# The down projection of a gated MLP as seven half-size products (Strassen), with weight sums made by accumulating transfers

## The chip, the cores and the metric

The kernel runs on one core of one Trainium2 chip. TensorE (PE) multiplies, VectorE (DVE), ScalarE (ACT) and GpSimd (POOL) do the element work, SyncE (SP) issues most of the transfers, and 16 DMA engines carry them. The metric is the device time of one execution in microseconds (us), the median of several runs.

## The reference

One layer of a hybrid decoder at 512 tokens and width 1024: a mixing sub-layer of four branches, then a gated MLP with a short convolution on its gate. The change lies in the MLP, and almost all of it in its last product:

```python
def conv_gated_mlp(h, w_up, conv_w, conv_b, w_down):
    up = h @ w_up                                   # 1024 -> 2 * 3072
    val = up[..., :D_FF]
    gate = causal_dwconv(up[..., D_FF:], conv_w, conv_b)
    return (val * jax.nn.gelu(gate)) @ w_down       # 3072 -> 1024

h = rms_norm(x, g_mlp_pre[l])
y = conv_gated_mlp(h, ...)
x = x + rms_norm(y, g_mlp_post[l])                  # the output
```

All data are fp32. The inputs and weights come from DRAM and the output goes back there.

## The kernel before

**Products in three passes.** A number is cut into a "hi" part that TensorE takes in one pass and a "lo" remainder. A product is hi by hi, hi by lo of the activations, and lo of the weights by hi of the activations, so one fp32 matmul is three matmuls of 128x128 by 128x512. A weight block of 128x1024 (512 KB) is fetched into `wraw` (`wfetch`, L72, on SP's queue), its hi part is copied by ACT (`whi`, L81), and DVE subtracts to give the lo part (`wlo`, L82). `split` does the same for an activation (L96 on ACT, L97 on DVE). `wraw`, `whi` and `wlo` have three buffers each.

**The up projection** (L791) is 48 units `upu(u)` of 24 matmuls. For each of 24 column chunks i there is a gate unit and a value unit; ACT and DVE do the convolution and the Gelu of the gate, DVE multiplies by the value (`fc`, L841), and `split` writes the activations `aT` (hi and lo, feature by token).

**The down projection** (L852) takes 24 weight blocks. Block 2p+nh holds the feature chunks 2p and 2p+1 (two halves of 512 columns in the block) of output half nh. 576 matmuls add into eight PSUM banks `acc[t, nh]`, one for each 128 tokens t and output half nh. The last four blocks are kept in `wl`, so that the four token tiles end one after another and the norm of one lies under the matmuls of the next.

**The norm and the output**: for each t two squares with sums on ACT (`fjk`, L881), a product with the gain (`fyg`, L877), the reciprocal root in small steps (L119 to L130), a scaled add to the residual (L887), and two stores (L888). The gain `gmo` is loaded once (L814).

Each engine works through its instructions in order, and a transfer waits in the order of the queue that issues it: SP's queue for the weights, POOL's for `gmo` and the two convolution constants. A scheduler has put each engine's instructions in an order, which can differ from that of the code.

Of the kernel before, what the change touches and what calls it, by code (L numbers as in the profile page):

```python
# [50 lines left out]
def _body(ctx, tc, nc, D):  # L51
# [758 lines left out]


    fp = fx.enter_context(pool("ff"))
    gmo = fp.tile([128, DM], F32, name="gmo")
    nc.gpsimd.dma_start(out=gmo, in_=D["g_mlp_post"])  # L814
    fcw = fp.tile([128, 24, 3], F32, name="fcw")
    fcb = fp.tile([128, 56], F32, name="fcb")[:, :24]
    nc.gpsimd.dma_start(out=fcw, in_=D["ffn_conv_w"])
# [26 lines left out]
    acc = {(t, nh): (mmb if nh == 0 else axb)("dn") for t in range(4) for nh in range(2)}  # L844

    def down(t, nh, kb, w, parts=(0, 1)):
        ts_ = slice(t * 128, (t + 1) * 128)
        for p in parts:
            for k in (2 * kb, 2 * kb + 1):
                cs = slice(k % 2 * 512, k % 2 * 512 + 512)  # L850
                for a in ((0,) if p else (0, 1)):
                    PE.matmul(acc[t, nh], aT[a][:, k, ts_], w[p][:, cs], start=(k == a == p == 0), stop=(k == 23 and p == 1))  # L852
# [14 lines left out]
    for t in range(4):
        for nh in range(2):
            for kb in (10, 11):
                down(t, nh, kb, W[kb, nh])  # L870
    for t in range(4):
# [409 lines left out]
```

## Time and profile before

| | us |
|---|---|
| median of 3 runs | 1184.91 (1182.65 to 1185.02) |
| the profiled execution | 1185.61 |
| its span, first to last instruction | 1183.8 |
| PE busy | 1163.4 (98%) |
| DVE busy | 687.7 (58%) |
| ACT busy | 522.8 (44%) |
| POOL busy | 124.6 (11%) |

The span is what the trace covers; 1.8 us of the profiled execution's time lie around it. PE is almost always busy, so a wait on another engine counts only if PE stands still for it.

### The profile page before, as it was taken

The page shows a single profiled execution, that of the slowest core. Times are in us where ns is not written, and L with a number is a line of the kernel's source. Part 1 is how long each engine was busy: PE and PEld are TensorE (multiplying, and loading weights), DVE is VectorE, ACT ScalarE, POOL GpSimd, SP SyncE. Part 2 cuts the span into 40 slices and gives each one's busy share as a digit, 9 for nine tenths or more (in the row PEclk, how much of TensorE's full clock was granted, in tenths as well). Part 3 has the DMA queues.
Part 4 walks back from the last instruction along what each step waited for, and adds up shares of the span by engine and source line. Part 5 has one row for each costly group of instructions (what it writes and reads, how often), then busy time and mean ns, then how long its engine had stood idle before and what let it go on. Part 6 is the DMA issues. An engine that isn't in the chain of part 4 may idle for free.

```text
span 1183.8 us, 15153 instructions
## 1 busy us (share of the span) xinstructions
PE 1163.4 (98%) x5786; PEld 969.0 (82%) x5786; DVE 687.7 (58%) x1249; ACT 522.8 (44%) x869; POOL 124.6 (11%) x163
## 2 busy tenths in 40 slices
PE   8999999998999999999999999999999999999997
PEld 8977788877788887888888888898888888888886
DVE  6857794588888534486447465585545444432224
ACT  6678734553434235443543234455444443422122
POOL 3000200196651000000000000010000000000000
PEclk9999999999999999999999999999999999999999
DMA  7612442213223322223122323713232323333221
GB/s 288 215 59 71 151 141 63 68 52 96 78 82 114 100 89 67 86 77 112 61 80 64 107 87 118 267 38 107 92 102 92 107 90 94 102 92 104 91 88 71
DMA packets 44296, 120.21 MB, mean 102 GB/s; under 512 B 9630, under 2 KB 13808, under 8 KB 44224
## 3 DMA queue, kind: packets, MB, share of 16 engines
q1 hardware_dynamic: 42432, 115.73, 30.1%
q0 software_dynamic: 1072, 2.46, 0.7%
q10 hardware_dynamic: 720, 1.06, 0.2%
q8 instruction: 45, 0.74, 0.2%
q14 instruction: 27, 0.22, 0.1%
HBM read 115.21 MB, written 4.01 MB: 101 GB/s over the span
## 4 chain that ended last, share of the span: by engine, by line
PE 88%; DVE 7%; DMA 1%; issue 1%; ACT 1%; POOL 1%; DVEq 0%; SPq 0%; ACTq 0%; POOLq 0%
PE up L791 22%; PE gate L90 12%; PE dn L852 11%; PE prj L90 7%; PE glu L90 4%; PE v L90 3%; PE k L90 3%; PE q L90 3%; PE xa L90 3%; PE us L90 3%; PE xq L90 3%; PE ga L90 3%; PE wo L711 2%; PE kv L267 1%; PE kv L90 1%
## 5 line engine op out<-in xcount | busy, mean ns | idle before, releaser
L82 DVE TENSOR_TENSOR wlo<-wraw,whi 128x1024 fp32r<-128x1024 f32 (+1 forms) x198 | 230.6, 1168 | 276.9 <-ACT whi L81 137.3
L81 ACT CAST whi<-wraw 128x1024 fp32r<-128x1024 f32 (+1 forms) x198 | 194.7, 986 | 332.0 <-PE dn L852 71.2
L791 PE MATMUL up<-h2l,whi 128*128 128x512 f32 (+1 forms) x400 | 148.9, 377 | 0.0
L791 PE MATMUL up<-h2h,whi 128*128 128x512 f32 (+1 forms) x400 | 148.7, 376 | 0.0
L90 PE MATMUL gate<-hTh,whi 128*128 128x512 f32 x256 | 101.1, 395 | 0.0
L90 PE MATMUL gate<-hTl,whi 128*128 128x512 f32 x256 | 100.5, 392 | 0.0
L791 PE MATMUL up<-h2h,wlo 128*128 128x512 f32 (+1 forms) x400 | 93.6, 376 | 0.0
L791 PEld LDWEIGHTS up<-h2l,whi 128*128 128x128 f32 x400 | 75.2, 188 | 13.9
L791 PEld LDWEIGHTS up<-h2h,whi 128*128 128x128 f32 x400 | 75.3, 188 | 13.8
L791 PEld LDWEIGHTS up<-h2h,wlo 128*128 128x128 f32 x400 | 72.3, 188 | 13.7
L90 PE MATMUL gate<-hTh,wlo 128*128 128x512 f32 x256 | 63.6, 389 | 0.0
L852 PE MATMUL dn<-whi,aTh 128*128 128x512 f32 x160 | 62.2, 389 | 0.0
L852 PE MATMUL dn<-whi,aTl 128*128 128x512 f32 x160 | 62.2, 389 | 0.0
L90 PEld LDWEIGHTS gate<-hTh,whi 128*128 128x128 f32 x256 | 48.1, 188 | 9.9 <-issue 0.5
L90 PEld LDWEIGHTS gate<-hTh,wlo 128*128 128x128 f32 x256 | 47.9, 188 | 9.8
L90 PEld LDWEIGHTS gate<-hTl,whi 128*128 128x128 f32 x256 | 48.1, 188 | 9.4
L841 DVE TENSOR_TENSOR fc<-fc,up 128x512 f32<-128x512 f32 x24 | 16.5, 687 | 57.6 <-PE up L791 56.5
L852 PE MATMUL dn<-wlo,aTh 128*128 128x512 f32 x160 | 39.5, 389 | 0.0
L290 DVE SCALAR_TENSOR_TENSOR th<-th,prj 128x512 f32<-128x512 f32 x24 | 16.4, 685 | 37.1 <-PE prj L90 36.8
L838 DVE SCALAR_TENSOR_TENSOR fc<-gs,fcw,fc 128x512 f32<-128x512 f32 x48 | 36.1, 751 | 1.5
L852 PEld LDWEIGHTS dn<-whi,aTl 128*128 128x128 f32 x160 | 30.0, 188 | 6.2
L852 PEld LDWEIGHTS dn<-wlo,aTh 128*128 128x128 f32 x160 | 30.0, 188 | 6.2
(517 smaller groups left out, 2439.9 us busy)
## 6 DMA issues: line engine op xcount, KB each, us to landing
wraw<-w_in SPq DMA_DIRECT2D x74, 512.0 KB, 3.5
wraw<-ffn_w_up SPq DMA_DIRECT2D x48, 512.0 KB, 3.4
wraw<-ffn_w_down SPq DMA_DIRECT2D x24, 512.0 KB, 3.5
wraw<-proj SPq DMA_DIRECT2D x24, 384.0 KB, 3.0
wraw<-ssm_glu SPq DMA_DIRECT2D x12, 384.0 KB, 3.0
wraw<-w_out SPq DMA_DIRECT2D x8, 512.0 KB, 4.3
wraw<-mem_wk SPq DMA_DIRECT2D x6, 512.0 KB, 6.8
wraw<-mem_wv SPq DMA_DIRECT2D x6, 512.0 KB, 4.2
```

What stands on the lines that cost most here:

```text
L81: cut[:] = (S.copy(hi[:, :n], raw[:, :n]), V.tensor_tensor(out=lo[:, :n], in0=raw[:, :n], in1=f32(hi[:, :n]), op=ALU.subtract))
L82: V.tensor_tensor(out=lo[:, :n], in0=raw[:, :n], in1=f32(hi[:, :n]), op=ALU.subtract))
L90: last = PE.matmul(out, a[:, k * 128:(k + 1) * 128], x[i][:, k], start=(n == 0), stop=(n == 3 * nk - 1))
L267: done = PE.matmul(bv[t][:, :256], mT[a][:, 4 * kh + k, t * 128:(t + 1) * 128], w[:, cs], start=(kh == k == o == 0 and a == 1), stop=(kh = ...
L290: V.scalar_tensor_tensor(out=th, in0=th, scalar=1.0, in1=b, op0=ALU.add, op1=ALU.mult)
L711: PE.matmul(b, mT[k][a][:, ts_], w[p][:, k % 2, :], start=(k == a == p == 0), stop=(k == 7 and p == 1))
L791: PE.matmul(b[:, cs], a[:, k * 128:(k + 1) * 128], x[:, k, cs], start=(n == k == 0), stop=(n == len(order) - 1 and k == KC - 1))
L838: V.scalar_tensor_tensor(out=c, in0=gs[:, j:j + 512], scalar=fcw[:, i, j:j + 1], in1=c, op0=ALU.mult, op1=ALU.add)
L841: V.tensor_tensor(out=c, in0=c, in1=bv, op=ALU.mult)
L852: PE.matmul(acc[t, nh], aT[a][:, k, ts_], w[p][:, cs], start=(k == a == p == 0), stop=(k == 23 and p == 1))
```

## The change

The activations are split in two halves of tokens and, within each pair of feature chunks p (12 pairs), in the even and the odd chunk; the weights likewise in the even and odd chunk and the two output halves. Of the eight half-size products of such a 2x2 scheme seven remain (Strassen in Winograd's form): P1 to P7, of 12 pairs x 2 token tiles x 3 passes = 72 matmuls each, 504 in all.

- **Order on PE.** Stage A: for each p, P5 and P7 with the weight sum `tb`, then P6 and P4 with the sum `ta` (24 matmuls, one "step"). Stage B: P1 (72 matmuls). Stage C: P3 and P2 (144 matmuls), the last three pairs held back and done token tile by token tile.
- **Weight sums.** With w0, w1 the two blocks of p and c0, c1 their even and odd halves, `tb` is loaded in two pieces (L896, L897) and then two transfers on POOL's queue add w1[c0] to each half of it (L901, `accum_op`), 256 KB each. The two pieces of `wraw` (L898, L899) are added on DVE to give `ta` (L902, L903). `tb` and `ta` are split as other weights are. Stages B and C load their weights in pieces of 256 KB again.
- **Activation sums** are made in the up projection: for each even and odd i together there are twelve DVE instructions, eleven of 256 columns and one of 512, where there were four of 512. Four parts of each p (512 KB) go to DRAM (`late`, L863, SP's queue) and come back into their place `SA` by a transfer on POOL's queue (L954) once step p of stage A has read it.
- **Memory.** The up projection's activations `h2` now lie in a pool of their own that is closed after it; the four buffers of `tb` for p of 1 and more lie there, so their loads begin when the last matmul of the up projection has read `h2`. `tb` of p = 0 and `wraw` of the first pairs use the old `wraw` buffers.
- `gmo` is loaded behind stage A. The output is put together from P1 to P7 by DVE adds and ACT copies; the last ones (L989, L992) stand ahead of the last two token tiles' norms.

```diff
     fp = fx.enter_context(pool("ff"))
-    gmo = fp.tile([128, DM], F32, name="gmo")
-    nc.gpsimd.dma_start(out=gmo, in_=D["g_mlp_post"])
...
-    aT = tuple(fp.tile([128, 24, L], F32R, name="aT" + s) for s in "hl")
+    a11, s2 = (fp.tile([128, 12, 256], F32, name=n) for n in ("a11", "s2"))
+    S3 = fp.tile([128, 12, 2, 256], F32R, name="S3")
+    SA = fp.tile([128, 12, 4, 256], F32R, name="SA")
+    late = [dp.tile([128, 4, 256], F32, name="late%d" % p) for p in range(12)]
...
-        V.tensor_tensor(out=c, in0=c, in1=bv, op=ALU.mult)
-        split(aT[0][:, i], aT[1][:, i], c)
+        p = i // 2
+        if i % 2 == 0:
+            V.tensor_tensor(out=a11[:, p], in0=c[:, :256], in1=bv[:, :256], op=ALU.mult)
+            V.tensor_tensor(out=c[:, 256:], in0=c[:, 256:], in1=bv[:, 256:], op=ALU.mult)
+            V.tensor_tensor(out=c[:, :256], in0=a11[:, p], in1=c[:, 256:], op=ALU.subtract)
+            split(S3[:, p, 0], S3[:, p, 1], c[:, :256])
+            a21 = c[:, 256:]
+        else:
+            V.tensor_tensor(out=c, in0=c, in1=bv, op=ALU.mult)
+            t4 = x1p.tile([128, 1024], F32R, tag="wel", name="t4").rearrange("p (s n) -> p s n", s=4)
+            split(SA[:, p, 2], SA[:, p, 3], c[:, 256:])
+            split(t4[:, 2], t4[:, 3], c[:, :256])
+            V.tensor_tensor(out=c[:, 256:], in0=c[:, 256:], in1=a21, op=ALU.subtract)
+            split(SA[:, p, 0], SA[:, p, 1], c[:, 256:])
+            V.tensor_tensor(out=s2[:, p], in0=c[:, 256:], in1=a11[:, p], op=ALU.add)
+            V.tensor_tensor(out=c[:, :256], in0=c[:, :256], in1=s2[:, p], op=ALU.subtract)
+            split(t4[:, 0], t4[:, 1], c[:, :256])
+            nc.sync.dma_start(out=late[p], in_=f32(t4))
...
-    for kb in range(10):
-        for nh in range(2):
-            w = wload(D["ffn_w_down"][kb * 2 + nh], 1024)
-            for p in (0, 1):
-                for t in range(4):
-                    down(t, nh, kb, w, (p,))
...
+    for p in range(12):
+        wd = (D["ffn_w_down"][2 * p], D["ffn_w_down"][2 * p + 1])
...
+            tb = dnp.tile([128, 1024], F32, tag="wtb", name="wtb", bufs=4)
+        nc.sync.dma_start(out=tb[:, c0], in_=wd[0][:, c0])
+        nc.sync.dma_start(out=tb[:, c1], in_=wd[1][:, c1])
+        nc.sync.dma_start(out=raw[:, c0], in_=wd[1][:, c1])
+        nc.sync.dma_start(out=raw[:, c1], in_=wd[0][:, c1])
+        for c in (c0, c1):
+            nc.gpsimd.dma_start(out=tb[:, c], in_=wd[1][:, c0], accum_op=ALU.add)
+        V.tensor_tensor(out=ta[:, c0], in0=tb[:, c0], in1=raw[:, c0], op=ALU.add)
+        V.tensor_tensor(out=ta[:, c1], in0=raw[:, c1], in1=ta[:, c0], op=ALU.add)
...
+        sa = halves(s2[:, p])
+        split(*wb_, tb)
+        prods(P5, [SA[:, p, x] for x in (0, 1)], wb_, c0, f, l)
+        prods(P7, [S3[:, p, x] for x in (0, 1)], wb_, c1, f, l)
+        split(*wa, ta)
+        prods(P6, sa, wa, c0, f, l)
+        prods(P4, [SA[:, p, x] for x in (2, 3)], wa, c1, f, l)
...
+    for p in range(12):
+        if p % 2 == 0:
+            w = wparts(D["ffn_w_down"][2 * p][:, c0], D["ffn_w_down"][2 * p + 2][:, c0])
+        if p > 5:
+            reload()
+        prods(P1, halves(a11[:, p]), w, (c0, c1)[p % 2], p == 0, p == 11)
...
+    for r in range(2):
+        for n, (b, a, w) in enumerate(rest):
+            prods(P3, b, w, c1, False, n == 2, (r,))
+        V.tensor_tensor(out=x22[r], in0=x22[r], in1=P3[r], op=ALU.add)
+        for n, (b, a, w) in enumerate(rest):
+            prods(P2, a, w, c0, False, n == 2, (r,))
+        V.tensor_tensor(out=s1[r], in0=s1[r], in1=P2[r], op=ALU.add)
+        final(r, (s1[r], x22[r]))
```

On POOL's queue the last three transfers of before stand at the end of its program; the gain, the taps and the bias of the convolution:

```order
L814 DMA gmo_7195<-g_mlp_post 128x1024
L817 DMA fcw_7197<-ffn_conv_w 128x72
L818 DMA fcb_7198<-ffn_conv_b 128x24
```

At the same place of the changed kernel the load of the gain is gone from its place (it comes back behind stage A), and 24 accumulating transfers and 12 reloads follow the two constants. The accumulating ones are those of L901, for p = 0 (`wraw_9113`) and p = 1 to 5 here (`x2`: one for each half); those of L954 bring `late` back into `SA`:

```order
L901 DMA wraw_9113<-ffn_w_down 128x512 x2
L901 DMA wtb_9160<-ffn_w_down 128x512 x2
L901 DMA wtb_9207<-ffn_w_down 128x512 x2
L954 DMA SA_7205<-late0_7206 128x1024
L901 DMA wtb_9254<-ffn_w_down 128x512 x2
L901 DMA wtb_9301<-ffn_w_down 128x512 x2
L901 DMA wtb_9348<-ffn_w_down 128x512 x2
L954 DMA SA_7205<-late1_7207 128x1024
L901 DMA wtb_9395<-ffn_w_down 128x512 x2
```

So the reload of p stands ahead of accumulating transfers of stage A, and waits there until step p is done.

On DVE, at the start of the down projection, before had the lo parts of weight blocks alone:

```order
L82 TENSOR_TENSOR wlo_9029<-wraw_9026,whi_9028 128x1024
L82 TENSOR_TENSOR wlo_9059<-wraw_9056,whi_9058 128x1024
L82 TENSOR_TENSOR wlo_9089<-wraw_9086,whi_9088 128x1024
L82 TENSOR_TENSOR wlo_9119<-wraw_9116,whi_9118 128x1024
```

Now the adds stand between them. Here `wtb_9160`, `wta_9159`, `wlo_9172` and `wlo_9170` belong to p = 1 (`wlo_9172` is the lo part of its `tb`, `wlo_9170` that of its `ta`), and `wtb_9207`, `wta_9206`, `wlo_9219`, `wlo_9217` to p = 2:

```order
L902 TENSOR_TENSOR wta_9206<-wtb_9207,wraw_9205 128x512
L97 TENSOR_TENSOR wlo_9172<-wtb_9160,whi_9171 128x1024
L902 TENSOR_TENSOR wta_9159<-wtb_9160,wraw_9158 128x512
L903 TENSOR_TENSOR wta_9206<-wraw_9205,wta_9206 128x512
L903 TENSOR_TENSOR wta_9159<-wraw_9158,wta_9159 128x512
L97 TENSOR_TENSOR wlo_9170<-wta_9159,whi_9169 128x1024
L97 TENSOR_TENSOR wlo_9219<-wtb_9207,whi_9218 128x1024
L97 TENSOR_TENSOR wlo_9217<-wta_9206,whi_9216 128x1024
```

The first add of p = 2, which reads the accumulated `wtb_9207`, stands ahead of the lo part that step 1 multiplies with.

In stage B, on DVE, the lo parts of `a11` (`asl`, two buffers, one for each of the 12 pairs) alternate with the lo parts of the weights, one for two pairs:

```order
L97 TENSOR_TENSOR asl_9742<-a11_7202,ash_9741 128x256
L97 TENSOR_TENSOR asl_9760<-a11_7202,ash_9759 128x256
L966 TENSOR_TENSOR x210_9681<-x210_9681,p6_9109 128x512
L966 TENSOR_TENSOR x211_9682<-x211_9682,p6_9110 128x512
L82 TENSOR_TENSOR wlo_9816<-wraw_9812,whi_9815 128x1024
L97 TENSOR_TENSOR asl_9771<-a11_7202,ash_9770 128x256
L97 TENSOR_TENSOR asl_9790<-a11_7202,ash_9789 128x256
```

So an `asl` of every second pair stands behind a `wlo` in the queue.

## Rows read from the trace of the kernel before

**Rows 1.** The page: span; busy time and share by engine; chain by engine.

```profile
span 1183.8 us, 15153 instructions
PE 1163.4 (98%) x5786; PEld 969.0 (82%) x5786; DVE 687.7 (58%) x1249; ACT 522.8 (44%) x869; POOL 124.6 (11%) x163
...
PE 88%; DVE 7%; DMA 1%; issue 1%; ACT 1%; POOL 1%; DVEq 0%; SPq 0%; ACTq 0%; POOLq 0%
```

**Rows 2.** Chain that ended last: start us, length us, its two last steps.

```profile
793.87 252.14 PE up L791 x1161
1046.01 130.57 PE dn L852 x576
```

**Rows 3.** Windows in up and down: length, busy us by engine, PEclk, DMA share, GB/s.

```profile
880.00:901.80 21.80, 21.80 (x98) 18.06 (x97) 10.47 (x15) 9.26 (x12) 0.00 (x0) 1.00 0.30 98
1060.00:1080.00 20.00, 20.00 (x90) 16.57 (x89) 4.90 (x4) 4.22 (x4) 0.00 (x0) 1.00 0.31 100
```

**Rows 4.** Groups by line and form from 790 us on: busy, mean ns, idle before.

```profile
L82 DVE TENSOR_TENSOR wlo<-wraw,whi 128x1024 fp32r<-128x1024 f32 x64 | 78.3, 1223 | 137.3 <-ACT whi L81 71.8 <-PE dn L852 63.2 <-PE up L791 2.2
L81 ACT CAST whi<-wraw 128x1024 fp32r<-128x1024 f32 x64 | 67.4, 1053 | 125.8 <-PE dn L852 71.2 <-PE up L791 54.5
...
L841 DVE TENSOR_TENSOR fc<-fc,up 128x512 f32<-128x512 f32 x24 | 16.5, 687 | 57.6 <-PE up L791 56.5 <-ACT fc L839 1.2
L97 DVE TENSOR_TENSOR aTl<-fc,aTh 128x512 fp32r<-128x512 f32 x24 | 16.4, 684 | 0.7 <-ACT aTh L96 0.7
...
L96 ACT CAST aTh<-fc 128x512 fp32r<-128x512 f32 x24 | 14.9, 622 | 34.3 <-DVE fc L841 34.3
```

**Rows 5.** Groups by form, whole span: weight splits of 256 columns.

```profile
L82 DVE TENSOR_TENSOR wlo<-wraw,whi 128x256 fp32r<-128x256 f32 x8 | 3.4, 424 | 11.1 <-PE gate L90 8.0 <-issue 3.0
...
L81 ACT CAST whi<-wraw 128x256 fp32r<-128x256 f32 x8 | 3.3, 407 | 12.5 <-PE gate L90 12.2 <-PE prj L90 0.4
```

**Rows 6.** Window while a 256 KB output store runs, columns as before.

```profile
1175.50:1176.20 0.70, 0.70 (x5) 0.56 (x3) 0.06 (x1) 0.00 (x0) 0.00 (x0) 1.00 1.04 386
```

**Rows 7.** DMA in 10 to 20 us: packets, MB, share of 16 engines.

```profile
q1 hardware_dynamic: 1130, 4.11, 102.0%
```

**Rows 8.** DMA issues: queue, count, KB each, median us to landing.

```profile
wraw<-ffn_w_down SPq DMA_DIRECT2D x24, 512.0 KB, 3.5
...
out_dram<-x SPq DMA_DIRECT2D x4, 256.0 KB, 2.1
...
ab<-ab POOLq DMA_DIRECT2D x2, 256.0 KB, 3.9
...
gmo<-g_mlp_post POOLq DMA_DIRECT2D x1, 512.0 KB, 3.7
```

**Rows 9.** Groups on POOL: the issue of a transfer there.

```profile
L487 POOL DMA_DIRECT2D ab<-ab x6 | 3.3, 551 | 133.6 <-DVE nmc L541 108.3 <-DVE z L1077 20.3 <-DVE KT L1136 5.0
```

**Rows 10.** Timeline of SP: start us, length of four issues.

```profile
1.18 1.85 SPq L201 DMA_DIRECT2D memT<-memT  x4
```

**Rows 11.** Timeline from 1176 us: the end of the kernel.

```profile
1176.66 0.60 ACT L881 ACTIVATE fjk<-dn 128x512 f32<-128x512 f32 x1 [2.03 <-PE dn L852]
...
1177.38 0.21 DVE L119 TENSOR_SCALAR fot<-cols 128x1 f32<-128x1 f32 x1 [1.82 <-ACT fjk L881]
1177.52 0.68 DVE L877 TENSOR_TENSOR fyg<-dn,gmo 128x512 f32<-128x512 f32 x1
1177.63 0.20 ACT L120 ACTIVATE foy<-fot 128x1 f32<-128x1 f32 x1 [0.28 <-DVE fot L119]
1178.11 0.15 DVE L123 RECIPROCAL foy<-foy 128x1 f32<-128x1 f32 x1
...
1180.43 0.33 SPq L888 DMA_DIRECT2D out_dram<-x  x1
```

**Rows 12.** Windows of 1 us near the start: columns as in the windows above.

```profile
7.00:8.00 1.00, 0.42 (x3) 0.33 (x3) 1.00 (x4) 1.00 (x4) 0.00 (x0) 1.00 1.03 383
...
9.00:10.00 1.00, 1.00 (x6) 1.00 (x6) 1.00 (x4) 0.83 (x2) 0.00 (x0) 0.50 1.02 418
...
11.00:12.00 1.00, 1.00 (x8) 1.00 (x8) 0.95 (x2) 0.77 (x2) 0.00 (x0) 0.72 1.03 422
```

More of the change, by code (lines that the diff above doesn't have):

```diff
@@ L687, in _body @@
     x1 = [x1[:, t] for t in range(4)]
-    h2 = tuple(x1p.tile([128, KC, L], F32R, tag="h2" + s, name="h2" + s) for s in "hl")
     cols = x1p.tile([128, 128], F32, name="cols")
+    h2x = ExitStack()
+    h2p = h2x.enter_context(pool("h2p", side="right"))
+    h2 = tuple(h2p.tile([128, KC, L], F32R, name="h2" + s) for s in "hl")
     with pool("wo") as wo:
@@ L840, in _body @@
         bv = upu(2 * i + 1)
-        V.tensor_tensor(out=c, in0=c, in1=bv, op=ALU.mult)
-        split(aT[0][:, i], aT[1][:, i], c)
-    S.sqrt(warm, warm)
[L844 to L852, printed above, removed]
@@ L867, in _body @@
[L867 to L871, printed above, removed]
+        p = i // 2
[16 more added lines that the diff above has]
+            nc.sync.dma_start(out=late[p], in_=f32(t4))
@@ new lines, in _body, with halves, prods @@
+    S.sqrt(warm, warm)
+    h2x.close()
+    dnp = fx.enter_context(pool("dn", side="right"))
+    def halves(src):
+        t = tuple(fp.tile([128, 256], F32R, tag="a" + x, name="as" + x, bufs=2) for x in "hl")
+        split(*t, src)
+        return t
+    def prods(banks, a, w, cs, first, last, rs=(0, 1)):
+        n = [0, 0]
+        for lo in (0, 1):
+            for r in rs:
+                for x in ((0,) if lo else (0, 1)):
+                    PE.matmul(banks[r], a[x][:, r * 128:(r + 1) * 128], w[lo][:, cs], start=(first and n[r] == 0),
+                              stop=(last and n[r] == 2))
+                    n[r] += 1
@@ L872, in _body, with final @@
+    gmo = x1p.tile([128, 1024], F32, tag="weh", name="gmo")
+    nc.gpsimd.dma_start(out=gmo, in_=D["g_mlp_post"])
+    side = lambda nm: [dnp.tile([128, 512], F32, name="%s%d" % (nm, r)) for r in range(2)]
+    u2, q7, x21, x22 = (side(n) for n in ("u2", "q7", "x21", "x22"))
+    for r in range(2):
+        S.copy(u2[r], P5[r])
+        S.copy(q7[r], P7[r])
+    def final(t, src):
         sc = cols[:, 8 + 2 * t:10 + 2 * t]
@@ L888, in _body, with wparts @@
             (nc.sync if nh else nc.scalar).dma_start(out=D["out"][t * 128:(t + 1) * 128, cs], in_=x1[t][:, cs])
+    def wparts(x, y):
+        raw = wp.tile([128, 1024], F32, tag="raw", name="wraw")
+        nc.sync.dma_start(out=raw[:, c0], in_=x)
+        nc.sync.dma_start(out=raw[:, c1], in_=y)
+        return wload(None, 1024, raw)
+    rest = []
+    P1, P3, P2 = ([f(n) for _ in range(2)] for n, f in (("p1", axb), ("p3", axb), ("p2", mmb)))
+    s1 = x1p.tile([128, 1024], F32, tag="wel", name="s1")
@@ new lines, in _body, with reload @@
+    s1 = [s1[:, c0], s1[:, c1]]
+    back = iter(range(12))
+    def reload():
+        p = next(back, None)
+        if p is not None:
+            nc.gpsimd.dma_start(out=SA[:, p], in_=late[p])
+    for p in range(12):
[4 more added lines that the diff above has]
+        prods(P1, halves(a11[:, p]), w, (c0, c1)[p % 2], p == 0, p == 11)
+        if p in (2, 3):
+            V.tensor_tensor(out=x21[p - 2], in0=q7[p - 2], in1=P4[p - 2], op=ALU.add)
+        elif p in (4, 5):
+            V.tensor_tensor(out=x22[p - 4], in0=P6[p - 4], in1=u2[p - 4], op=ALU.subtract)
+        elif p in (6, 7):
+            V.tensor_tensor(out=x21[p - 6], in0=x21[p - 6], in1=P6[p - 6], op=ALU.subtract)
@@ new lines, in _body @@
+    for r in range(2):
+        S.copy(s1[r], P1[r])
+    for p in range(12):
+        w = wparts(D["ffn_w_down"][2 * p][:, c1], D["ffn_w_down"][2 * p + 1][:, c1])
+        reload()
+        b, a = ([SA[:, p, x] for x in y] for y in ((0, 1), (2, 3)))
+        if p < 9:
+            prods(P3, b, w, c1, p == 0, False)
+            prods(P2, a, w, c0, p == 0, False)
+        else:
+            rest.append((b, a, w))
+        if p in (1, 2):
+            r = p - 1
+            V.tensor_tensor(out=x22[r], in0=x22[r], in1=s1[r], op=ALU.subtract)
+            V.tensor_tensor(out=x21[r], in0=x21[r], in1=s1[r], op=ALU.add)
+            V.tensor_tensor(out=u2[r], in0=x22[r], in1=q7[r], op=ALU.subtract)
+        if p in (3, 6):
+            final(2 + p // 6, (x21[p // 6], u2[p // 6]))
@@ L889, in _body @@
+    for r in range(2):
+        for n, (b, a, w) in enumerate(rest):
[5 more added lines that the diff above has]
+        final(r, (s1[r], x22[r]))
     fx.close()
```

26 lines of the change are left out of this document (14 added, 12 removed).

## The prediction

> **What bounds the kernel now.** I read the page first: PE is busy for 98% of the span, and the chain that ended last is PE for 88% [rows 1]. DVE's 58% and ACT's 44% therefore cost something only where PE stands still for them. The chain's last steps say where the change acts: the up projection is one unbroken run of matmuls for 252.14 us, the down projection another for 130.57 us [rows 2]. So in both stages PE alone sets the time; 130.57 / 576 = 0.2267 us for one matmul. The windows show what is free beside it: per 21.8 us of the up projection DVE works 10.47 us and ACT 9.26; in 20 us of the down projection DVE works 4.9, ACT 4.2, and the DMA engines are 31% busy with 100 GB/s [rows 3]. A stage that gives PE less to do and the others more has to be judged by what these three then need.
>
> **Saved: matmuls.** 576 − 504 = 72 matmuls of the same shape, 72 x 0.2267 = **−16.3 us**. A step of stage A (24 matmuls) takes 5.44 us, twelve of them 65.3, stage B 16.3, stage C 32.6.
>
> **The up projection: 0.** For two chunks i DVE did 2 x 0.687 (L841) and 2 x 0.684 (lo parts) [rows 4]; now one of 0.687 and eleven of 256 columns, which the lo part of a 128x256 weight block prices at 0.424 [rows 5]. That is 5.35 in place of 2.74, so 10.47 + 2.6 = 13.1 us of 21.8. ACT makes five hi parts of 0.407 [rows 5] in place of two of 0.622 [rows 4], +0.8. Each store of 512 KB adds some 1.3 us of DMA time to engines that are 30% busy. PE's next unit needs none of this, only a free PSUM bank, which the multiply at the head of the chain frees as before; the 8 us that DVE still has idle are the cover. If it were gone, the 12 pairs would cost up to 2.6 us each; at 60% I see no reason.
>
> **Stage A: DVE and ACT have room.** A step needs on DVE two adds of 0.684, two lo parts of 1.223 and one of 0.424 = 4.2 us of 5.44; on ACT two copies of 1.053 and one of 0.407 = 2.5 [rows 4, 5].
>
> **Stage A: the transfers.** This is what decides. 256 KB at 386 GB/s, with all 16 engines busy (share 1.04), are 0.68 us of everything the DMA engines have [rows 6]; 4.11 MB in 10 us at 102% make 1.27 us for 512 KB [rows 7]. From the last matmul of the up projection (call it T; only then may `tb` of p ≥ 1 be loaded) until the accumulation for p = 11 has landed, these have to pass: 22 pieces of `tb` (15.0 us), 16 pieces of `wraw` for p = 4 to 11 (10.9), seven reloads that stand ahead in POOL's queue (8.9), the last `late` store (1.3), and 22 accumulating transfers. The first four make 36.1 us. The trace of before has no accumulating transfer. Its lower bound is a copy, 0.68 us (it cannot move less than its 256 KB), so 15.0 in all. It must however read the addend from DRAM and the old value from SBUF, 512 KB read for 256 KB written: the 512 KB row gives 1.27, twice the copy 1.36. An upper bound is three passes of a copy, 2.04. I take 1.27 to 1.36, since the row of 512 KB is the nearest to reading twice: 28 to 30 us, and 64 to 66 us in all.
>
> When is it needed? DVE, in the queue shown for step 1 and likewise later, makes the adds of p+2 ahead of the lo part of step p+1's `tb`. So step 10's third pass waits for the accumulation of p = 11, two adds and one lo part (2.6 us), and one landing (2.1 us for 256 KB on SP's queue [rows 8], of which 0.68 was counted). Step 10 would start at T + 54.4 and has 0.9 us of hi matmuls ahead; so the transfers must be done by about T + 51.4. Add 1 us in which the DMA engines idle after T (nothing can be accumulated before the first piece has landed). Lateness: copy 51.1 + 1 − 51.4 ≈ 0.7; at 1.27, 13.7; at 1.36, 15.6. I take **+14.6 us**. Most of it would show as PE waiting for `wlo` of the next step, spread over stage A.
>
> The Trainium skill has a rule on this, on the page "Collectives: The Full Stack", section "The bandwidth ceiling: the fold count and why AG ≠ RS ≠ AR": a reduce reads two sources for one write and was measured at about half of the copy's rate (62.28 against 32.35). That is for collectives; no run here shows it. By it alone an accumulating transfer is an estimated 1.3 us and the sum stays at about +2.5; by the copy's row it would be −5.9.
>
> **The transition into stage A** is part of this lateness when the transfers bind; with cheap ones it stands alone. At T SP issues `tb` for p = 1 and 2, 0.46 us apart [rows 10]; the third piece has landed at about T + 3.5 (2.1, then 0.68 for each further). POOL issues for 0.55 us [rows 9], and a 256 KB transfer of its queue took 3.9 us to land against 2.1 on SP's [rows 8]: T + 7.4. DVE's add of p = 2 (0.68), which stands ahead of step 1's `wlo_9172` (1.22), ends that at T + 9.3; PE wants it at 5.44 + 0.9 = T + 6.3. That is a wait of 3.0. Behind `wlo_9172` stand three adds (2.0) and ACT's copy (1.05), so `ta` is ready at T + 12.4, where PE has come to its products at 9.3 + 1.8 = 11.1: 1.3 more, and 0.4 for its lo part: 4.7. PE's granted clock fell to 0.50, 1.2 GHz of 2.4, two windows after one with PE busy for 0.42, and was at 0.72 two windows later [rows 12]; here the matmuls behind the first wait are partly covered by the second. With that and the hand-offs I take 6.2.
>
> **Stage B.** DVE has six weight lo parts (7.3), eleven `asl` (4.7) and eight adds of 512 (5.5): 17.5 us beside 16.3 of PE, so at least 1.2 late, and every second `asl` stands behind a lo part of 1.22 with only two buffers: up to some 5. I take **+3.0**. Stage C has one lo part in 2.72 us of matmuls: 0; the last five reloads (6.4 us) have stage B for it.
>
> **The end.** Before, ACT's last square started 0.08 us after the last matmul (1046.01 + 130.57 = 1176.58 [rows 2], 1176.66 [rows 11]) and DVE went on at 1177.38. Now an add out of PSUM (0.68, as `fyg`) comes first, and both squares follow it in series, 0.7 to 0.8 more. Before, `fyg` of 0.68 held the reciprocal back by some 0.28 (it started at 1178.11, where ACT's root had ended at 1177.83 [rows 11]); that now stands elsewhere. **+1.2 us**. The two stores and their landing stay (last issue at 1180.43 [rows 11]). `gmo`, 3.7 us from issue [rows 8], comes behind stage A and is needed 20 us later: 0.
>
> **Sum**: −16.3 + 14.6 + 3.0 + 1.2 = +2.5 on the profiled 1185.6 (0.7 above the median, within the runs), so **1188 us**.
>
> **Rivals.** (A) *The accumulating transfer costs hardly more than a copy.* Then stage A needs 51 us of transfers in 65 and only the transition is left: −16.3 + 6.2 + 3.0 + 1.2 = −5.9, **1180 us**. For it: engines that read and write at once might take the second read along, and nothing in the trace says they don't. Against: twice the bytes are read, and at full share time went with bytes [rows 6, 7]. It decides where 51.1 + 22(a − 0.68) − 50.4 = 12.1, at a = 1.20 us, 1.8 copies: just under my value. (B) *It costs nearly three copies, or POOL's queue is late in handing out its packets*: at 1.87 us for one the transfers take 77 us, the lateness is 26.8, the sum +14.7, **1200 us**. For it speaks POOL's queue landing 1.8 us later than SP's for the same 256 KB [rows 8]; against, POOL has nothing else to do, and 0.55 us an issue is far below 1.3. The page "SBUF — State Buffer" of the Trainium skill, in its note on the "DVE blocks DMA" trap, lets DVE copies in a two-port mode starve such a queue; the DVE work of stage A is adds and subtractions, which it does not count among them, and no run here shows it. (C) *Nothing waits*: the scheduler's order leaves slack that I have not seen, the clock holds, stage B hides: −16.3 + 1.2 + at most 3 ≈ −12, **1174 us**. Against it stands the first accumulation at T, which cannot land before about T + 6.
>
> **How the numbers follow.** The measurement tells some 0.2% (2.4 us) from no change. Forecast (accumulating costs 1.6 to 2.3 copies, 1184 to 1193): 0.46; A (below, 1179 to 1184): 0.31; B (1194 to 1204): 0.18; C: 0.05. Faster by over 0.2% (below 1182.5): most of A, and C, 0.34; within: 0.18 from the edge of A and the lower third of the forecast; slower: 0.48. The range takes A and half of B in: 1178 to 1201. The forecast's own is 1184 to 1193.
>
> **What would show it.** The down stage at 504 matmuls of about 0.227 us busy; in stage A a DMA share near 1 with PE waiting for `wlo` in most steps from 1 to 10, and the accumulating transfers on POOL's queue at twice a copy's packet time. With A the share would be near 0.8 and all waiting at step 1. Stage B should show short waits for `asl`, 1 to 5 us together, the end from the last matmul to the last instruction 1.2 us longer, and the up projection unchanged at 252 us. A longer up projection, or waits in stage C, would make me wrong for a cause not counted here.

## The result: 0.6% slower, and where the time went

The changed kernel takes 1190.84 us (median of 4 runs, 1189.92 to 1191.29) against 1184.95 of before: a ratio of 1.0059, 95% interval 1.0047 to 1.0071. That lies in the range and on the side that was forecast, 3 us above the point. The range went from 1178 to 1201 us and held faster kernels as well as slower ones, so being inside it says little; that the time also lies in the forecast's own 1184 to 1193 says more.

The page of the profile after, its busy times by engine and its DMA queues (packets, MB, share of 16 engines' span); `q0` is POOL's:

```profile
PE 1155.6 (97%) x5714; PEld 958.0 (81%) x5714; DVE 767.7 (65%) x1427; ACT 559.4 (47%) x953; POOL 152.5 (13%) x199
...
q1 hardware_dynamic: 52800, 131.47, 33.8%
q0 software_dynamic: 6256, 15.05, 5.1%
```

In before the chain ran through one unbroken row of matmuls up to the last of them [rows 2]. Now the chain that ended last has transfers in it (its long steps: start, length, step):

```profile
792.03 252.17 PE up L793 x1161
1050.56 8.36 DMA wtb<-ffn_w_down
1076.17 9.30 DMA wtb<-ffn_w_down
1090.97 7.74 DMA wtb<-ffn_w_down
1104.57 19.76 PE p L881 x78
1139.55 33.39 PE p L881 x145
```

The up projection still takes 252.17 us, so its activation sums cost nothing. What PE waited for in the down projection is in its timeline (start, length, form; in brackets the idle time before and what ended it):

```profile
1044.02 1.07 PE L881 MATMUL p<-whi,SA 128*128 128x512 f32 x4
...
1058.06 2.07 PE L881 MATMUL p<-whi,SA 128*128 128x512 f32 x4 [8.37 <-ACT whi L96]
...
1085.06 0.73 PE L881 MATMUL p<-wlo,SA 128*128 128x512 f32 x2 [0.83 <-DVE wlo L97]
...
1104.57 1.18 PE L881 MATMUL p<-wlo,SA 128*128 128x512 f32 x2 [2.27 <-DVE wlo L97]
...
1127.39 0.39 PE L881 MATMUL p<-whi,ash 128*128 128x512 f32 x1
...
1132.62 0.73 PE L881 MATMUL p<-whi,asl 128*128 128x512 f32 x2 [0.41 <-DVE asl L97]
...
1179.01 0.39 PE L881 MATMUL p<-wlo,SA 128*128 128x512 f32 x1
```

Stage A runs from 1044.02 to 1127.39 (its end is the first matmul of stage B): 83.4 us for 288 matmuls, 18.1 more than 288 x 0.2267. Of that, from the same timeline, step 0 to step 1 lost 8.6, step 1 another 3.1 (on a halved clock), step 5 1.2, step 6 0.5, step 8 4.2 (2.27 of waiting and again matmuls on a slow clock, 0.58 on the mean from 1104 to 1108). Steps that did not wait took 5.51 us as well, not 5.44. Stages B and C took 52.0 us, 3.0 over 216 x 0.2267. From the last matmul's end (1179.40) to the end of the span (1189.0) are 9.6 us; before it was 7.2 (1176.58 to 1183.8). So the down projection and the end got −16.3 + 18.1 + 3.0 + 2.4 = 7.2 us longer. In these two executions the up projection ended 2.0 us earlier after (1044.02 against 1046.01 [rows 2]), which makes the spans differ by 5.2 only; in the other profiled kernels here it ended between 1042.8 and 1045.1 though the code of their up projection is the same, so this shift is not taken for an effect of the change.

The windows (length, busy us by engine, PEclk, DMA share, GB/s) show the transfers at their limit through stage A, and the clock in the first wait:

```profile
1046.00:1118.00 72.00, 60.18 (x240) 47.10 (x240) 43.10 (x59) 26.74 (x33) 24.93 (x33) 0.91 1.08 307
...
1050.00:1055.00 5.00, 0.00 (x0) 0.00 (x0) 0.00 (x0) 0.00 (x0) 3.99 (x5) 0.84 1.06 274
1055.00:1060.00 5.00, 1.94 (x5) 1.56 (x6) 1.06 (x2) 1.04 (x1) 0.91 (x2) 0.50 1.12 282
```

The DMA share stands at 1.08 for 72 us, where before had 0.31 [rows 3]; but only 307 GB/s are counted, against 386 to 422 at full share [rows 6, 12]; the experiment with two loads below shows where the rest is. DVE was busy for 43 of the 72 us, so its sum of work isn't the bound. With PE standing still the granted clock fell to 0.50, 1.2 GHz, and PE's first products after the wait ran at that.

### The profile page after: what moved, and what is told of

Its sections match the earlier page's. It is cut to its first block, busy times and chain, and to the rows that moved or that the text cites. A ratio compares the mean times of both kernels' runs of the same rounds, so it can differ in the third digit from the quotient of the medians.

```text
span 1189.0 us, 15579 instructions
## 1 busy us (share of the span) xinstructions
PE 1155.6 (97%) x5714; PEld 958.0 (81%) x5714; DVE 767.7 (65%) x1427; ACT 559.4 (47%) x953; POOL 152.5 (13%) x199
## 4 chain that ended last, share of the span: by engine, by line
PE 86%; DVE 5%; DMA 5%; issue 2%; ACT 1%; POOL 1%; SPq 0%; DVEq 0%; POOLq 0%; ACTq 0%
PE up L793 22%; PE gate L90 14%; PE prj L90 8%; PE p L881 5%; PE glu L90 4%; DMA wtb<-ffn_w_down 4%; PE v L90 3%; PE k L90 3%; PE q L90 3%; PE xa L90 3%; PE us L90 3%; PE xq L90 3%; PE ga L90 3%; PE wo L713 2%; PE kv L267 1%
## 5 line engine op out<-in xcount | busy, mean ns | idle before, releaser
L82 DVE TENSOR_TENSOR wlo<-wraw,whi 128x1024 fp32r<-128x1024 f32 (+1 forms) x196 | 228.0, 1167 | 177.2 <-ACT whi L81 80.4
L881 PE MATMUL p<-whi,SA 128*128 128x512 f32 x192 | 53.9, 396 | 8.4 <-ACT whi L96 8.4
L881 PEld LDWEIGHTS p<-whi,SA 128*128 128x128 f32 x192 | 36.4, 190 | 16.7 <-ACT whi L96 8.8
L763 POOL TENSOR_TENSOR xn<-xn,gpr 128x512 f32<-128x512 f32 x2 | 3.4, 1701 | 275.3 <-ACT xn L762 275.3
L843 DVE SCALAR_TENSOR_TENSOR fc<-gs,fcw,fc 128x512 f32<-128x512 f32 x48 | 36.1, 751 | 1.7
L881 PE MATMUL p<-wlo,SA 128*128 128x512 f32 x96 | 32.0, 405 | 3.3 <-DVE wlo L97 3.1
L844 ACT ACTIVATE fc<-fc 128x512 f32<-128x512 f32 x24 | 15.2, 632 | 40.1 <-DVE fc L843 40.1
L901 POOL DMA_DIRECT2D wraw<-ffn_w_down x2 | 1.8, 1065 | 232.1 <-DMA wraw<-ffn_w_down 232.1
```

What stands on the lines that cost most here:

```text
L82: V.tensor_tensor(out=lo[:, :n], in0=raw[:, :n], in1=f32(hi[:, :n]), op=ALU.subtract))
L763: G.tensor_tensor(out=tt, in0=tt, in1=gpr[:, cs], op=ALU.mult)
L881: PE.matmul(banks[r], a[x][:, r * 128:(r + 1) * 128], w[lo][:, cs], start=(first and n[r] == 0), stop=(last and n[r] == 2))
L901: nc.gpsimd.dma_start(out=tb[:, c], in_=wd[1][:, c0], accum_op=ALU.add)
```

## The experiments

The table gives for each run the ratio to before with its interval, and from its PE timeline the length of stage A, of stages B and C, and of the stretch from the last matmul to the end of the span (without any wait at 0.2267 us a matmul: 65.3 and 49.0 us).

| run | ratio | A | B + C | end |
|---|---|---|---|---|
| before (130.57 in all) | 1 | | | 7.2 |
| the change | 1.0059 [1.0047, 1.0071] | 83.4 | 52.0 | 9.6 |
| e1_plain | 0.9995 [0.9986, 1.0005] | 75.4 | 52.7 | 9.6 |
| e2_two_loads | 1.0053 [1.0038, 1.0068] | 81.7 | 52.8 | 9.6 |
| e3_reload_late | 1.0038 [1.0024, 1.0053] | 78.5 | 55.3 | 9.6 |
| e4_dve_sums | 1.0022 [1.0013, 1.0032] | 78.7 | 51.6 | 9.6 |
| e5_early_tb1 | 1.0027 [1.0017, 1.0037] | 78.9 | 52.2 | 9.6 |
| e6_three_asl | 1.0061 [1.0043, 1.0079] | 85.3 | 49.9 | 9.6 |
| e7_squares_first | 1.0059 [1.0044, 1.0074] | 83.0 | 51.9 | 8.6 |
| e8_best | 0.9882 [0.9867, 0.9896] | 66.1 | 49.8 | 8.6 |
| e9_acc_placed | 1.0010 [1.0001, 1.0019] | 76.9 | 51.9 | 9.6 |
| e10_acc_placed_late | 1.0004 [0.9994, 1.0014] | 73.9 | 56.3 | 9.6 |

The median of before was 1183 to 1185 us over these sets of runs, so ratios are compared, not times. For each run the three lengths, less 130.57 + 7.2, give its difference to before within 1.5 us; the table holds nearly all that changed.

**What an accumulating transfer costs.** In e1 it is a plain load:

```diff
-            nc.gpsimd.dma_start(out=tb[:, c], in_=wd[1][:, c0], accum_op=ALU.add)
+            nc.gpsimd.dma_start(out=tb[:, c], in_=wd[1][:, c0])
```

> The 24 accumulating transfers become plain loads of the same 256 KB on the same queue, behind the same waits (the weight sum tb is therefore not made, the data are those of one addend). Theory (an accumulating transfer takes the DMA engines about two copies, and in stage A the DMA engines are the bound): some 22 x 0.7 = 15 us of DMA time go; the waits at steps 5, 6 and 8 (1.2 + 0.5 + 4.2 us) vanish and the first two (8.6 + 3.1) shrink to about 6, so about 11 us less, near 1180 us. Rival 1 (the bound is the chain load, POOL issue, landing, whatever the transfer does): 1190 +- 2 us, the same waits. Rival 2 (DVE's order, the adds of p+2 ahead of the lo part of p+1, is the bound): also 1190 +- 2 us.

Measured: 7.6 us off (1.0059 to 0.9995 of 1184), all in stage A, where the theory had 11 and both rivals none. The waits at steps 5, 6 and 8 are gone, as the theory had it. The losses at steps 0 and 1 fell by 2.2 us only (9.5 us in place of 11.7) and not to 6: there an effect other than the accumulate is at work. PE's first wait in e1:

```profile
1056.79 2.07 PE L881 MATMUL p<-whi,SA 128*128 128x512 f32 x4 [6.37 <-ACT whi L96]
```

POOL's queue and SP's over 72 us of stage A, in the change and then in e1 (packets, MB, share of 16 engines):

```profile
q0 software_dynamic: 4444, 10.43, 61.5%
q1 hardware_dynamic: 6262, 11.66, 46.3%
```

```profile
q1 hardware_dynamic: 6475, 12.05, 48.4%
q0 software_dynamic: 3457, 12.00, 47.3%
```

In e1 POOL's 12.00 MB took 0.473 x 72 = 34.1 us of the 16 engines, 2.84 us a MB or 0.74 for 256 KB. In the change 10.43 MB took 44.3 us. Of these, 5.77 MB are the 22 accumulating transfers; the other 4.66 MB at 2.84 are 13.2 us; so the 22 took 31.1 us, **1.41 us each, 1.9 times a plain load**.

In e2 each of them becomes two plain loads:

```diff
-            nc.gpsimd.dma_start(out=tb[:, c], in_=wd[1][:, c0], accum_op=ALU.add)
+            cp1 = nc.gpsimd.dma_start(out=tb[:, c], in_=wd[1][:, c0])
+            if p:
...
+                with tc.issue_after(cp1.ins):
+                    nc.gpsimd.dma_start(out=dum[:, :512], in_=wd[1][:, c0])
```

> Each accumulating transfer of p >= 1 becomes two plain loads of 256 KB, one into its place and one, right behind it in POOL's queue, into a tile that nobody reads (the weight sum is not made). Theory (an accumulate costs its two reads): the DMA engines get the same work as with accumulates, and the time lies within 3 us of the change, 1188 to 1194 us. Rival (the adding itself, not the second read, is dear, or POOL's chain sets the time): as with one plain load each, near 1180 us, or clearly above 1194 us because POOL has twice as many transfers to issue at 0.9 us each.

Measured: 1.0053, within 1 us of the change, stage A 81.7 in place of 83.4. Two plain loads and one accumulate are worth the same here. POOL had 22 transfers more to issue, so its issuing is not what binds. The bytes say so too. In the same 72 us the change and then e2 moved:

```profile
DMA packets 10710, 22.14 MB, mean 307 GB/s; under 512 B 1189, under 2 KB 1189, under 8 KB 10706
```

```profile
DMA packets 10978, 27.79 MB, mean 386 GB/s; under 512 B 1532, under 2 KB 1532, under 8 KB 10974
```

With the 5.77 MB of the accumulating transfers counted a second time the change comes to 27.9 MB, or 388 GB/s: the rate of full share, and e2's.

**What shares the DMA engines.** In e3 the reloads stand behind the last accumulate:

```diff
-            nc.gpsimd.dma_start(out=tb[:, c], in_=wd[1][:, c0], accum_op=ALU.add)
+            lastacc = nc.gpsimd.dma_start(out=tb[:, c], in_=wd[1][:, c0], accum_op=ALU.add)
...
-            nc.gpsimd.dma_start(out=SA[:, p], in_=late[p])
+            with tc.issue_after(lastacc.ins):
+                nc.gpsimd.dma_start(out=SA[:, p], in_=late[p])
```

> The same kernel with the reloads of SA ordered behind the last accumulating transfer in POOL's queue, so none of them runs in stage A before step 9. Theory (DMA time binds stage A): seven reloads of 512 KB (1.3 us each) leave it, the later waits (steps 5, 6, 8, 5.9 us together) go, the transition gets about 1 us shorter: 1183 to 1185 us, unless stage C then waits for its reloads. Rivals 1 and 2 (a chain or DVE's order): unchanged, 1190 +- 2 us.

Measured: stage A got 4.9 us shorter, with only one short wait left behind step 1 (0.56 us), as the theory had it; the first wait stayed (8.33 us), where it had 1 us less. Stages B and C got 3.3 longer, in new waits for `ash` and `asl`: on ACT and DVE these stand behind the parts of a weight that landed 7.6 us after its issue. The step of the chain, and PE's wait:

```profile
1118.97 7.59 DMA wraw<-ffn_w_down
```

```profile
1128.06 0.74 PE L881 MATMUL p<-whi,ash 128*128 128x512 f32 x2 [1.67 <-ACT ash L96]
```

The ratio fell by 0.0021 only, which misses the expected 1183 to 1185 us by 3 us or more. The transfers were in the way, and most of what their move gave was lost again where they were put.

**Sums on DVE.** In e4 nothing accumulates; each weight is loaded once:

```diff
-        nc.sync.dma_start(out=raw[:, c0], in_=wd[1][:, c1])
+        nc.sync.dma_start(out=raw[:, c0], in_=wd[1][:, c0])
...
-            nc.gpsimd.dma_start(out=tb[:, c], in_=wd[1][:, c0], accum_op=ALU.add)
+                V.tensor_tensor(out=tb[:, c0], in0=tb[:, c0], in1=raw[:, c0], op=ALU.add)
+                V.tensor_tensor(out=ta[:, c0], in0=tb[:, c0], in1=tb[:, c1], op=ALU.add)
+                V.tensor_tensor(out=tb[:, c1], in0=tb[:, c1], in1=raw[:, c0], op=ALU.add)
+                V.tensor_tensor(out=ta[:, c1], in0=raw[:, c1], in1=ta[:, c0], op=ALU.add)
```

> No accumulating transfer: w0[c0], w1[c1], w1[c0], w0[c1] are each loaded once and DVE makes all four adds, those of p placed behind the lo part of step p-1's tb. Theory: the DMA engines need 4 x 0.72 + 1.3 = 4.2 us a step, DVE 4 x 0.684 + 2 x 1.223 + 0.42 = 5.6 against 5.44 of PE, so DVE binds a little: 12 x 0.16 = 2 us, and the transition some 5: stage A stands about 7 us in place of 18, near 1180 us. Rival 2 (DVE already sets stage A): not faster, or slower than 1190 us.

Measured: 1.0022, where 1180 us, a ratio of 0.996, was expected; faster than the change, so rival 2 is out as the whole cause. Steps 2 to 9 ran without a wait, 5.5 us each, with 5.6 us of DVE work expected in them; but the first wait was 8.7 us, as long as ever, with no accumulate in the kernel. Two of the theory's three parts held; the transition did not.

**The transition.** In e5 only `tb` of p = 1 moves:

```diff
-        if p == 0:
+        if p < 2:
             tb = wp.tile([128, 1024], F32, tag="raw", name="wraw")
```

> Of the change only the place of tb for p = 1 is another: a wraw buffer, as for p = 0, so that its loads and its two accumulating transfers lie in the up projection and not behind its last matmul. Theory of the first wait (8.4 us): step 1's tb is summed too late because its loads, its accumulates and the prefetched loads of later pairs share the DMA engines from T on; with it made before T the first wait (whi of p = 1) goes. Step 1's second product still needs ta of p = 1, whose buffer the last store of late (landed 12 us after T) frees, so some 6 us of the 11.7 stay: 1184 to 1186 us. Rival (the first wait is not that transfer, but ACT or DVE being late after the up projection): unchanged, 1190 +- 2 us.

Measured: 1.0027, 1 to 2 us above what was expected; the first wait is gone, so it was that transfer, and a second of 7.4 us stands where step 1 comes to `ta`. PE's wait, and DVE's adds before it (for p = 2, then for p = 1):

```profile
1058.90 0.80 PE L881 MATMUL p<-whi,ash 128*128 128x512 f32 x1 [7.37 <-ACT whi L96]
```

```profile
1054.49 0.69 DVE L902 TENSOR_TENSOR wta<-wtb,wraw 128x512 f32<-128x512 f32 x1 [5.09 <-DMA wtb<-ffn_w_down]
...
1056.29 0.69 DVE L902 TENSOR_TENSOR wta<-wraw 128x512 f32<-128x512 f32 x1 [0.39 <-DMA late<-t]
```

`ta` of p = 1 has the buffer (`wel`) in which the last `t4` lay, so its first add waits for the last store of `late`; issued at 1049.09, that had landed only now, 7.1 us later, where these stores took 2.7 us on the median. But two things held this add. DVE's order puts the adds of p = 2 ahead of it, and they waited 5.09 us for the accumulates of p = 2; when they were done, the store was the later by 0.39 us only. To mend one of the two alone would have gained little.

In e4 the times point to the store. There the first add into `ta` of p = 1 (L905) stands on DVE between the adds that make `tb`:

```profile
1056.88 0.69 DVE L905 TENSOR_TENSOR wta<-wtb 128x512 f32<-128x512 f32 x1 [5.09 <-issue]
```

The profile names no releaser for it (`issue`), but the store, issued at 1051.48, took 5.3 us to land, to 1056.8. PE waits for the copy of the `tb` that the next add (L906) completes.

In the change itself the chain of the first wait reads so (SP's issue of `tb`, POOL's accumulates of p = 1 and the first of p = 2, ACT's copy, DVE's add for p = 2, the lo part of p = 1):

```profile
1044.26 0.33 SPq L896 DMA_DIRECT2D wtb<-ffn_w_down  x1
...
1047.46 1.73 POOL L901 DMA_DIRECT2D wtb<-ffn_w_down  x2 [23.89 <-DMA wtb<-ffn_w_down]
...
1050.56 0.86 POOL L901 DMA_DIRECT2D wtb<-ffn_w_down  x1 [1.36 <-DMA wtb<-ffn_w_down]
...
1056.96 1.04 ACT L96 CAST whi<-wtb 128x1024 fp32r<-128x1024 f32 x1 [8.22 <-DMA wtb<-ffn_w_down]
...
1058.94 0.69 DVE L902 TENSOR_TENSOR wta<-wtb,wraw 128x512 f32<-128x512 f32 x1 [9.74 <-DMA wtb<-ffn_w_down]
...
1059.55 1.22 DVE L97 TENSOR_TENSOR wlo<-wtb,whi 128x1024 fp32r<-128x1024 f32 x1
```

Here the store did not bind: it took 7.6 us from 1048.80 and had landed at 1056.4, and the add into `ta` of p = 1 came at 1060.68. What bound was the accumulates of p = 1. Issued from 1047.5 on, they had landed at 1056.9, up to 9 us later; a 256 KB transfer of this queue took 3.9 us in before [rows 8]. While they were under way the DMA engines also carried `tb` of p = 2 and 3, the last store, the next `tb`, a reload and accumulates of later p.

**All of it mended, with and without accumulates.** e8 takes the sums by DVE in place, `ta` in the raw tile itself, `tb` of p = 1 in the buffer this frees (loaded in the up projection), three `ash` and `asl`, and the squares of e7:

```diff
-        ta = x1p.tile([128, 1024], F32, tag=("weh", "wel")[p % 2], name="wta")
+        ta = raw
...
+        elif p == 1:
+            tb = x1p.tile([128, 1024], F32, tag="weh", name="wtb")
...
+                V.tensor_tensor(out=tb[:, c0], in0=tb[:, c0], in1=tb[:, c1], op=ALU.add)
+                V.tensor_tensor(out=tb[:, c1], in0=tb[:, c1], in1=raw[:, c0], op=ALU.add)
+                V.tensor_tensor(out=raw[:, c0], in0=raw[:, c0], in1=tb[:, c0], op=ALU.add)
+                V.tensor_tensor(out=raw[:, c1], in0=raw[:, c1], in1=raw[:, c0], op=ALU.add)
```

> Sums on DVE with each weight read once: tb is loaded as w0[c0], w1[c0], wraw as w1[c1], w0[c1], four adds in place, ta made in wraw itself (no buffer shared with the stores of late), tb of p = 1 in the buffer that ta leaves free and loaded during the up projection, adds of p behind the lo part of step p-1, three ash and asl buffers, squares as in the run before. Theory: DMA 4.2 us and DVE 5.6 us a step of 5.5, so stage A stands 1 to 4 us in place of 18, stage B about 1 to 3, the end 8.3 in place of 7.2: -16.3 + 3 + 2 + 1 + 0.8 (steps of 5.51) = about -9.5 against before: near 1174 us, ratio 0.992. Rival (the transition's stall has another source than the transfers and the shared buffer): a first wait of 5 us or more stays, ratio 0.996 or above.

Measured: 1169.66 us (1169.52 to 1169.80), ratio 0.9882, 1.2% faster than before and 4 us better than expected, since stages A and B do not wait at all. Its window over ten steps, and the last long step of its chain, one run of matmuls from the up projection on:

```profile
1050.00:1105.00 55.00, 55.00 (x242) 45.00 (x241) 51.51 (x71) 26.07 (x31) 5.45 (x11) 1.00 0.85 280
```

```profile
1043.64 111.69 PE p L881 x486
```

DVE is busy for 94% of that stretch and the DMA share is 0.85: this version is close to DVE's limit, and no longer at the transfers'.

e9 mends the transition in the same way but keeps the accumulates, and has the two `ash` and `asl` buffers and the squares of the change; e10 also puts the reloads behind them (by the edit of e3).

```diff
+        ta = raw
...
-            nc.gpsimd.dma_start(out=tb[:, c], in_=wd[1][:, c0], accum_op=ALU.add)
+            lastacc = nc.gpsimd.dma_start(out=tb[:, c], in_=wd[1][:, c0], accum_op=ALU.add)
-        V.tensor_tensor(out=ta[:, c0], in0=tb[:, c0], in1=raw[:, c0], op=ALU.add)
-        V.tensor_tensor(out=ta[:, c1], in0=raw[:, c1], in1=ta[:, c0], op=ALU.add)
+                V.tensor_tensor(out=raw[:, c0], in0=raw[:, c0], in1=tb[:, c0], op=ALU.add)
+                V.tensor_tensor(out=raw[:, c1], in0=raw[:, c1], in1=raw[:, c0], op=ALU.add)
```

> The change with its accumulating transfers kept, but the transition mended as in the run that beat both kernels: ta is made in wraw itself (no buffer shared with late), tb of p = 1 lies in the buffer that this frees and is summed before the last matmul of the up projection, adds of p behind the lo part of step p-1. Theory (DMA time binds stage A; the first waits are only where the missing time shows first): 4.3 us of transfers leave the stretch behind T, so stage A still stands 13 to 15 us in place of 18, now spread over the later steps, as waits for wlo: 1185 to 1187 us, ratio 1.002 to 1.004. Rival (the transition is a loss of its own, beside the later waits of 6 us): stage A stands 5 to 7 us, 1178 us, ratio 0.995.

> As the run above, with the reloads ordered behind the last accumulating transfer. Theory: seven to eight reloads (some 9 to 10 us of DMA time) leave stage A, which then stands 4 to 6 us; stage B waits some 2 us more for weights behind the reloads, as when the reloads were moved alone: about 1180 us, ratio 0.996 to 0.999. Rival (the reloads do not matter once the transition is mended): the same time as the run above within 1.5 us.

Measured, e9: stage A 76.9 us, 11.6 over its matmuls, and the missing time now shows in several places of PE's timeline:

```profile
1060.26 1.42 PE L881 MATMUL p<-whi,SA 128*128 128x512 f32 x4 [4.20 <-ACT whi L96]
...
1095.21 0.73 PE L881 MATMUL p<-wlo,ash 128*128 128x512 f32 x2 [1.52 <-DVE wlo L97]
1102.21 0.74 PE L881 MATMUL p<-wlo,ash 128*128 128x512 f32 x2 [1.26 <-DVE wlo L97]
1108.81 0.73 PE L881 MATMUL p<-wlo,ash 128*128 128x512 f32 x2 [0.83 <-DVE wlo L97]
```

That is 1.4 us under the 13 to 15 that the theory gave (its ratio, 1.002 to 1.004, was missed from below by 0.001), and 4.6 over the upper end of the rival's 5 to 7. e10: stage A 3 us shorter, stages B and C 4.4 longer, the time unchanged (1.0004 against 1.0010, intervals overlapping), as its rival had it, but not because the reloads do not matter. Its window over stage B, and POOL's queue in it (2.97 MB, over five reloads), show them at work beside the matmuls that wait:

```profile
1112.00:1135.00 23.00, 19.56 (x74) 14.30 (x73) 13.71 (x20) 10.98 (x19) 1.06 (x2) 0.93 0.78 277
```

```profile
q0 software_dynamic: 824, 2.97, 34.5%
```

Of e10 the expected ratio (0.996 to 0.999) was missed: stage A kept 8.6 us in place of 4 to 6 (4.8 of it a wait for `whi` at p = 2, like that of p = 1 in the change), and stages B and C lost more than the 2 us foreseen.

**Stage B and the end.** e6 gives `ash` and `asl` three buffers (`bufs=3` for `bufs=2` in `halves`); e7 turns the squares of the last two token tiles:

```diff
-        for nh in range(2):
+        for nh in nhs:
...
-        final(r, (s1[r], x22[r]))
+        final(r, (s1[r], x22[r]), (1, 0))
```

> Of the change only the buffers of ash and asl are three in place of two. Theory of stage B: its waits (3 of 0.4 us named, about 3 us in all against 504 matmuls without a wait) come from a loop of ash, whi, wlo and asl through two buffers; with three the loop opens and stage B gets 1.5 to 3 us shorter. Rival (DVE's 17.5 us of work beside 16.3 us of matmuls set it): stage B changes by less than 0.7 us.

> Of the change only the order of the two squares of the last two token tiles is another: that of x22, which is ready earlier, first, then that of s1. The time from the last matmul to the end of the span was 7.2 us before and 9.6 now. Theory: 1.3 us of it is the last add standing in DVE's queue behind the third tile's norm, and 0.7 the second square in series; with the order turned the third tile's norm starts 0.7 us earlier and the last tile has one square behind its add: 8.0 to 8.6 us in place of 9.6. Rival (the stores at the end set it): unchanged 9.6.

Measured: in e6 stage B's waits vanish (B and C 49.9 in place of 52.0 us), so a loop through two buffers made them and not DVE's load. The chain of the change shows the loop's steps one after another, 3.5 us for 2.7 us of matmuls:

```profile
1132.62 0.75 PE p L881 x2
...
1133.39 1.06 ACT whi L81
...
1134.47 1.22 DVE wlo L82
1135.70 0.35 DVE asl L97
...
1136.09 0.74 PE p L881 x2
```

But e6's stage A stood 1.9 us longer in its profiled execution and its median isn't better. Whether the third buffer, which stage A uses too, does that, or whether waits on a full DMA system just vary so much from one execution to the next, is open; stage A of e7, where nothing of it was touched, differs by 0.4 us from the change. In e7 the end takes 8.6 us in place of 9.6, as expected; its median cannot show 1 us.

## Why the prediction was right, point by point

- **Matmuls saved, −16.3 us:** nearly. Without any wait (e8) 504 matmuls took 115.93 us (stage A 66.08, B and C 49.85), 14.64 less than 130.57; the mean matmul is 0.2300 us in place of 0.2267, in this mix of operands. 1.7 us of the term were not there.
- **The up projection, 0:** right (252.14 to 252.17), with DVE at 12.6 us of 21.8 where 13.1 was worked out.
- **An accumulating transfer at 1.27 to 1.36 us:** nearly; 1.41 by the queues' shares, and e2 shows it worth two loads. The Trainium skill's rule ("Collectives: The Full Stack", section "The bandwidth ceiling: the fold count and why AG ≠ RS ≠ AR") that a reduce goes at about half of the copy's rate, stated there for collectives, agrees with these runs: 1.9 against its 62.28/32.35 = 1.93.
- **Stage A late by 14.6 us:** 18.1 (17.3 without the slower matmuls). The mechanism, DMA engines full for 72 us, was right, and most of the difference is the price: with 1.41 the text's own sum is 36.1 + 31.0 + 1 − 51.4 = 16.7 (its 51.4 comes to 51.3 when its terms are added up). That it comes so near is partly luck, for the place was wrong. The text had the time fixed by `wlo` of step 10, which was ready 1.6 us before PE came to it (1115.7 and 1117.3); the last wait of stage A stood in step 8. What was mis-sized is the **transition**: it was taken as a part that stands alone with 6.2 us, from landing times of quiet queues (2.1 and 3.9 us), and as contained in the lateness otherwise. On full queues the same transfers took up to 9 us to land, so 11.7 us are lost before any later step is late, and 9.5 still with plain loads (e1). The text put most waits into steps 1 to 10 as `wlo`; two thirds of the loss came with the wait for `whi` of step 1 and the slow clock behind it.
- **A wait that the text did not have:** `ta` of p = 1 shares a buffer with the last store of `late`. It did not bind in the change, but it stood ready behind the accumulates: by the times shown for e4 it kept the first wait at 8.7 us there, where nothing accumulates.
- **Rival A (accumulates as cheap as copies, 1180 us):** refuted, and its price too: with copies (e1) the kernel is only as fast as before, since the transition stays at 9.5 and not 6.2.
- **Stage B, +3.0:** 3.0 for B and C, the waits 2.2 of it, but by the loop through two buffers and not by DVE's sum of work.
- **The end, +1.2:** 2.4. The term that was missing is DVE's order: the last add (L992) could start at 1179.4 and started at 1180.70, behind the third tile's two scaled adds:

```profile
1179.37 1.41 DVE L937 SCALAR_TENSOR_TENSOR x<-fyg,for,x 128x512 f32<-128x512 f32 x2
...
1180.70 0.68 DVE L992 TENSOR_TENSOR s<-s,p 128x512 f32<-128x512 f32 x1
```

So −14.64 + 17.29 + 2.16 + 2.38 = +7.2 by the runs, against +2.5 forecast; 1190.84 − 1184.95 is 5.9. Three of the four terms came out above the forecast and one below it.

## What to carry to other kernels

When a change trades matmuls for transfers, count the DMA engines' time per step, with an accumulating transfer as two loads (so it was here, 256 KB from DRAM into SBUF), and compare it with the step. Here four loads, two accumulates and a reload make 4 x 0.74 + 2 x 1.41 + 1.5 = 7.3 us, and that did not hide in 5.5; moved into the next stage, the transfers cost most (e3) or all (e10) of the gain there. At a stage's start take landing times of full queues, not of quiet ones, and look for buffers that the stage before still has to store from. Where an engine has room, reading each weight once and adding there can beat adding on the way: the same seven products ran 1.2% faster than before once DVE made the sums in place, the transition was mended, and the third buffer and the turned squares were in. No one of these edits did it alone (e4 to e7, e9).

## What was not expected of the hardware

- On POOL the record of an accumulating transfer's issue is 0.86 us long (median), that of a plain one of the same size 0.54. The row of the change, and that of e1 (their means):

```profile
L901 POOL DMA_DIRECT2D wtb<-ffn_w_down x22 | 19.7, 946 | 61.1 <-DMA wtb<-ffn_w_down 47.2 <-DVE wlo L97 6.7 <-DVE wta L902 6.2
```

```profile
L901 POOL DMA_DIRECT2D wtb<-ffn_w_down x22 | 11.9, 540 | 59.8 <-DMA wtb<-ffn_w_down 45.0 <-DVE asl L97 7.4 <-ACT ash L96 5.1
```

That POOL is held so much longer is not shown: where issues follow one another in the change, the next one starts 0.54 us after, and the plain reload behind an accumulate has a record of 0.88 us as well:

```profile
1051.86 0.85 POOL L901 DMA_DIRECT2D wtb<-ffn_w_down  x1 [0.45 <-issue]
1052.40 0.88 POOL L954 DMA_DIRECT2D SA<-late  x1
```

- A step of 24 matmuls without any wait took 5.51 us where 24 matmuls of the old order took 5.44. The extra lies in P6 and P4 (1.40 and 1.39 us in step 2, P5 and P7 1.37 and 1.35); why was not tried.
